# The wide two-operand operations of GpSimd in a two-layer block, moved to VectorE

## The chip, the cores and the metric

The kernel runs on one core of a Trainium2 chip. The metric is the time of one execution on the device in microseconds (us). The engines are named as the profile names them: PE is TensorE (its weight loads are listed apart as PEld), DVE is VectorE, ACT is ScalarE, POOL is GpSimd, SP is SyncE, which issues the DMAs of this kernel.

## The reference

The reference computes two layers over 1024 tokens of width 1024, in float32. Each layer has a mixing part and a gated feed-forward part; each part is normalised before and after, and scaled, shifted and gated by vectors that come from a conditioning vector `c`.

```python
for layer in range(DEPTH):                       # 2
    shift, scale, gate = adaln_params(c, ada_w[layer, 0], ada_b[layer, 0])
    h = rms_norm(x, norm_pre[layer, 0]) * (1.0 + scale) + shift
    if layer % 2 == 0:
        y = delta_rwkv_mixer(h, ...)             # 4 gated-delta heads of 128, 8 RWKV-7 heads of 64
    else:
        y = rglru_mixer(h, ...)                  # a gated linear recurrence of width 1024
    x = x + gate * rms_norm(y, norm_post[layer, 0])
    ...
    y = swiglu_ffn(h, ffn_w_gate[layer], ffn_w_up[layer], ffn_w_down[layer])   # width 2816
    x = x + gate * rms_norm(y, norm_post[layer, 1])
```

In the delta mixer a triangular system of a chunk is solved for every head; the kernel does it by a product form of the inverse.

## The kernel before

**Split products.** PE's fast float32 product rounds its operands. So each operand that needs the full precision is kept as two tiles, a rounded one (`wh`, `xh`) and the rest (`wl = w - wh`), and a product is three matmuls: `wh*xh + wh*xl + wl*xh`. A weight tile of 128 x 512 therefore takes a DMA (`wf` or `wd`), a copy on ACT that rounds (`nc.scalar.copy(wh, wf)`, line 144) and a two-operand subtraction (line 145 in `load_w`). Lines 677 and 678 in `parts` do the same in the feed-forward part.

**Who subtracts.** In `load_w` it is POOL while `self.pool_lo` is set: 2 during the whole mixer (every tile), True in the recurrence `lru` (only tiles with `k0 > 0`); else DVE. Weights that come a second time (the second half of the tokens) are not split again: the two parts were written to DRAM (`self.pd`) and are read back by DMA. In the feed-forward part `first(f)` gives its two splits to POOL, all other `parts` go to DVE.

**The mixer** (`mixer`): two halves of 512 tokens, and in each 8 groups of heads. A group goes through three stages (`inputs`, `first`, `second`), and the stages of three neighbouring groups are issued together, by counts. Every `first` calls `inverse` once. There, `L`, `Z` (lines 1198, 1200) are made on DVE, `X` is copied on POOL (line 1202), and `im = first + one32` is a sum on POOL (line 1204). `im` is used once, after the last level of the inverse. In the first half weights come in and are split; in the second half they are read back. `mix_out` for the first half is issued at step `MIX0`, inside the second half.

**The feed-forward part** (`ffn`): for each of 22 blocks `f` of the hidden width, seven products of 12 matmuls in the manner of Strassen. `first(f)` makes the two products that need only `ffn_w_gate`; some of them are made ahead, before and while `operands` prepares the sums and differences of the activations on DVE and ACT. Then `rest` goes through the blocks: `second(f)`, `first(f+1)`, `third(f)`.

**Order.** Only the start of the program fixes the order on DVE and PE by hand. In all else the order of instructions on each engine is made by a planner from the order of the program, the dependences, free buffers and the durations that it expects. On the chip each engine then runs its own list strictly in that order.

Of the kernel before, what the change touches and what calls it, by code (L numbers as in the profile page):

```python
# [15 lines left out]
ALU = mybir.AluOpType  # L16
# [56 lines left out]
class Block:  # L73
# [53 lines left out]
    def load_w(self, w, c0, nk=KD, n=128, tag=None, key=None):  # L127


        nc = self.nc  # L130
        step = 512 // n
        out = []
        for k0 in range(0, nk, step):
            m = min(step, nk - k0)
            wh = self.t(tag or "wh", [128, step, n], F32R)[:, :m]
            wl = self.t(tag or "wl", [128, step, n], F32R)[:, :m]
            kept = self.wparts.get((key, c0, k0))
            if kept is not None:
                for x, r in zip((wh, wl), kept):
                    nc.sync.dma_start(x.bitcast(F32).rearrange("p k c -> p (k c)"), r)  # L140
            else:
                wf = self.t(next(self.wtags), [128, step, n])[:, :m]
                nc.sync.dma_start(wf, w[k0 * 128:(k0 + m) * 128, c0:c0 + n].rearrange("(k p) c -> p k c", p=128))
                nc.scalar.copy(wh, wf)  # L144
                (nc.gpsimd if self.pool_lo and (self.pool_lo > 1 or k0) else nc.vector).tensor_tensor(wl, wf, wh, ALU.subtract)  # L145
                if key is not None:
                    kept = []
                    for x in (wh, wl):
                        r = self.pd[len(self.wparts) * 256 + len(kept) * 128:][:128, :m * n]
                        nc.sync.dma_start(r, x.bitcast(F32).rearrange("p k c -> p (k c)"))  # L150
                        kept.append(r)
                    self.wparts[key, c0, k0] = kept
            out += [(wh[:, k], wl[:, k]) for k in range(m)]
        return out
# [38 lines left out]
    def run(self):  # L193
        nc, a = self.nc, self.a
        self.pools = {}
        self.bg = iter(())
        self.abufs = iter(())
        self.held = False
        self.wtags = cycle(("wf",))
        self.pool_lo = False  # L200
        self.c = self.pool("const")
        main = self.pool("main")
        self.tags(main, wf=2, wh=3, wl=3, ht=16, yx=9, sm1=6, ss=8, e=8, jk=1)
        psum = self.pool("psum", PSUM)
        self.tags(psum, mm=2, es=1, sa=3, sb=2)
        x1, x2, x3, mT = [self.dram(n) for n in ("x1", "x2", "x3", "mT")]
        self.gd = self.dram("gd", 2 * NF * 2 * 128, 512)
        self.pd = self.dram("pd", 132 * 256, 512)
        self.wparts = {}
        self.cd = self.dram("cd", 2 * (PRE + MID) * 128, 512)  # L210
        with ExitStack() as self.ctx:
            self.tags(self.pool("start"), a0=6, k0=12, k1=1, wab=1)
            E = mybir.EngineType
            with self.tc.manual_schedule(engines={E.DVE, E.PE}):
                hs, AB, others = self.start()
            others()
            self.setup_constants()
            self.mixer_params(a["mix_w_in"][0])
        with ExitStack() as self.ctx:
            self.tags(self.pool("work"), p=12, ar=2, s1=8, cy=12, s2=4, st=2, gb=2, ad=4)  # L220
            rest = self.ctx
            with ExitStack() as self.ctx:
                self.tags(self.pool("mix"), W=2, h16=5, ch=4, sg=2, gp=4, egc=3, **{f"S{i}": 1 for i in range(8)})
                hs, AB, late = self.mixer(a["x"][0], x1, mT, hs, AB)
            self.ctx = rest
            self.tags(self.pool("deep"), wd=6)
            self.layers(hs, AB, x1, x2, x3, late)
# [431 lines left out]
    def ffn(self, l, hs):  # L659
# [4 lines left out]
        nc, a = self.nc, self.a  # L664
# [4 lines left out]
        flat = lambda x: x.rearrange("p k c -> p (k c)")  # L669
        b11, b21 = hs[:4], hs[4:]  # L670
        b22, t1, t2, t3, t4 = ([] for _ in range(5))
        kept = {}

        def parts(full, eng=None):
            wh = self.t("wh", [128, 4, 128], F32R)
            wl = self.t("wl", [128, 4, 128], F32R)
            nc.scalar.copy(flat(wh), full)  # L677
            (eng or nc.vector).tensor_tensor(flat(wl), full, flat(wh), ALU.subtract)  # L678
            return wh, wl

        def product(ps, w, xs, start):
            wh, wl = w
            for k in range(4):
                xh, xl = xs[k]
                self.mm(ps, wh[:, k], xh, start=start and k == 0, stop=False, more=not start)
                self.mm(ps, wh[:, k], xl, start=False, stop=False, more=not start)
                self.mm(ps, wl[:, k], xh, start=False, stop=k == 3, more=not start)
# [10 lines left out]
        def first(f, away=False):  # L698

            a11, a12 = fetch("ffn_w_gate", f)  # L700
            pa = self.t("mm", [128, 512])
            product(pa, parts(a11, nc.gpsimd), b11, True)
            c1 = E()
            nc.scalar.copy(c1, pa)  # L704
            product(pa, parts(a12, nc.gpsimd), b21, False)
            s0 = E()
            self.act(s0, pa, AF.Silu)
            kept[f] = [(lambda x=x: x) for x in (c1, s0)]
            if away:
                for n, x in enumerate((c1, s0)):  # L710
                    nc.sync.dma_start(self.cpart(f, n), x)
                    kept[f][n] = lambda n=n: self.back(f, n)
# [82 lines left out]
        def rest(ahead, late):  # L795
            following(0)
            for f in range(NF):
# [4 lines left out]
                if f >= late:  # L802
                    self.tick()

        return first, operands, rest

    def cpart(self, f, n):
# [89 lines left out]
    def layers(self, hs, AB, x1, x2, x3, late):  # L897
# [4 lines left out]
        for n, (l, x_in, x_out) in enumerate(subs):  # L902
# [7 lines left out]
            if l is not None:  # L910
                first, operands, rest = self.ffn(l, hs)
# [12 lines left out]
            for h in range(2):  # L924
                keep = h == 1 and l is None
                if l is None:
                    self.pool_lo = True
                    ys, w = self.lru(h, hs)
                    self.pool_lo = False
                    lhs = lambda k, half: ys[k]  # L930
                else:
                    w = self.a["ffn_w_down"][l]
                    for f in range(AHEAD if h == 0 else 0):
                        gs[0, f] = self.load_g(0, f)

                    def lhs(k, half):
                        if half == 0 and h == 0 and k + AHEAD < NF:
                            gs[0, k + AHEAD] = self.load_g(0, k + AHEAD)
                        g = gs[h, k]
                        if half == 1 and h == 0 and k >= 2:  # L940
                            gs[1, k - 2] = self.load_g(1, k - 2)
                        return g

                    if h == 1:
                        for f in (NF - 2, NF - 1):
                            gs[1, f] = self.load_g(1, f)
                nxt = []

                def aside():
                    if h == 0:  # L950
                        if l is None:
                            nxt.append(self.prenorm(x_in, 1, *AB))
                    elif n + 1 < len(subs):
                        while "A" not in res[n + 1] or n == 0 and len(res[1]["G"]) < 2:
                            self.tick()
                        nxt.append((res[n + 1]["A"], res[n + 1]["B"]))
                        nxt.append(self.prenorm(x_out, 0, *nxt[0]))

                last = n + 1 == len(subs) and h == 1
                xs = self.down(lhs, w, h, x_in, x_out, res[n]["G"], F_BANKS[4:] + F_BANKS[:4],  # L960
                               "s2" if keep else "yx", ("cy", 6) if keep else ("ht", 7) if last else (None, 0), keep, aside,
                               "lru" if l is None else None)
                if nxt:
                    hs = nxt[-1]
                    if h:
                        AB = nxt[0]


    def mixer(self, x, x_out, mT, hs, AB):
        nc, a, c = self.nc, self.a, self.c  # L970
# [5 lines left out]
        self.gW, self.rW = self.t("W", [128, 4, 128], F16), self.t("W", [128, 8, 64], F16)  # L976
        for W in (self.gW, self.rW):
            nc.gpsimd.memset(W, 0.0)
        self.pool_lo = 2
        groups = [(h, i) for h in range(2) for i in (0, 4, 1, 5, 2, 6, 3, 7)]  # L980
        one, two = {}, {}
        half = {}
# [22 lines left out]
        for n in range(len(groups) + 2):  # L1005
# [23 lines left out]
            for kind, res in zip(kinds, self.together(tasks)):  # L1029
                if kind == 1:  # L1030
                    two[n - 1] = res
                elif kind == 0:
                    one[n] = res
        self.pool_lo = False
        return hs, AB, lambda: self.mix_out(1, x, x_out, mT, r0["G"], F_BANKS)

    def mix_out(self, h, x, x_out, mT, Gb, banks):
# [148 lines left out]
    def inverse(self, lev, tri, first, one16, one32, ones, prod, shape, W, turn):  # L1186
# [6 lines left out]
        nc = self.nc  # L1193
# [7 lines left out]
        X = self.t("h16", shape, F16)  # L1201
        nc.gpsimd.tensor_copy(X, one16)
        im = self.t("s1", shape)
        nc.gpsimd.tensor_tensor(im, first, one32, ALU.add)
        for n in range(len(lev)):
            nb, s = N >> (n + 1), 1 << n
            runs = lambda x, e: x.rearrange("p c (b e s) -> p c b e s", e=2, s=s)[:, :, :, e]
# [366 lines left out]
```

## Time and profile before

| | |
|---|---|
| time of three runs | 2735.04, 2748.76, 2749.45 us, median 2748.76 |
| profiled execution | 2738.0 us, span 2736.2 us, mean granted TensorE clock 0.989 |
| PE, PEld | 2618.2 us (96% of the span), 2030.5 us (74%) |
| DVE, ACT, POOL | 1814.0 us (66%), 1178.8 us (43%), 336.9 us (12%) |

The span runs from the first to the last instruction; 1.8 us of the profiled time lie around it. Busy time is the union of an engine's instructions; PE's ends are modelled, so that a busy PE may still be waiting inside. In the order of the span: the start (to about 50 us), the mixer's first half of tokens (to about 450), its second half with the output product of the first (to about 960), the feed-forward of layer 0 (to about 1700), the recurrence (to about 2020), the feed-forward of layer 1.

### The profile page before, as it was taken

The page shows a single profiled execution, that of the slowest core. Times are in us where ns is not written, and L with a number is a line of the kernel's source. Part 1 is how long each engine was busy: PE and PEld are TensorE (multiplying, and loading weights), DVE is VectorE, ACT ScalarE, POOL GpSimd, SP SyncE. Part 2 cuts the span into 40 slices and gives each one's busy share as a digit, 9 for nine tenths or more (in the row PEclk, how much of TensorE's full clock was granted, in tenths as well). Part 3 has the DMA queues.
Part 4 walks back from the last instruction along what each step waited for, and adds up shares of the span by engine and source line. Part 5 has one row for each costly group of instructions (what it writes and reads, how often), then busy time and mean ns, then how long its engine had stood idle before and what let it go on. Part 6 is the DMA issues. An engine that isn't in the chain of part 4 may idle for free. (4 is left out here: it accounts for less than half of the span.)

```text
span 2736.2 us, 44054 instructions
## 1 busy us (share of the span) xinstructions
PE 2618.2 (96%) x16104; PEld 2030.5 (74%) x16104; DVE 1814.0 (66%) x3376; ACT 1178.8 (43%) x2164; POOL 336.9 (12%) x288
## 2 busy tenths in 40 slices
PE   6899999999999998999999999999998999999998
PEld 3666667676766666788888878777876888888887
DVE  5677777668776655997664473995855976664233
ACT  3555564554455525333332233573645333332222
POOL 2332220002111113000110000210012001110000
PEclk9999999999999999999999999999999999999999
DMA  7644442336832374775448884889655754448753
GB/s 244 225 132 140 139 154 79 110 105 231 274 107 83 97 250 157 247 233 188 135 148 306 300 273 140 293 299 299 201 197 166 227 178 148 135 135 289 247 177 110
DMA packets 423327, 519.60 MB, mean 190 GB/s; under 512 B 32667, under 2 KB 217790, under 8 KB 423110
## 3 DMA queue, kind: packets, MB, share of 16 engines
q1 hardware_dynamic: 423110, 516.78, 57.2%
q8 instruction: 127, 2.08, 0.3%
q14 instruction: 90, 0.74, 0.1%
HBM read 367.76 MB, written 148.90 MB: 189 GB/s over the span
## 5 line engine op out<-in xcount | busy, mean ns | idle before, releaser
L98 PE MATMUL mm<-ht,wh 128*128 128x512 f32 x1920 | 656.6, 415 | 19.1 <-ACT e L704 15.8
L98 PEld LDWEIGHTS mm<-ht,wh 128*128 128x128 f32 x1920 | 351.7, 191 | 107.7 <-ACT e L704 26.8
L98 PE MATMUL mm<-ht,wl 128*128 128x512 f32 x960 | 389.9, 408 | 11.4 <-DMA wl<-pd 5.9
L145 DVE TENSOR_TENSOR wl<-wd,wh 128x512 fp32r<-128x512 f32 x156 | 107.5, 690 | 177.9 <-ACT wh L144 175.7
L98 PEld LDWEIGHTS mm<-ht,wl 128*128 128x128 f32 x960 | 183.1, 191 | 55.0 <-DMA wl<-pd 6.8
L144 ACT CAST wh<-wd 128x512 fp32r<-128x512 f32 x168 | 104.4, 622 | 268.5 <-PE sb L98 216.9
L144 ACT CAST wh<-wf 128x512 fp32r<-128x512 f32 x133 | 82.3, 622 | 166.1 <-PE sb L98 78.5
L145 POOL TENSOR_TENSOR wl<-wf,wh 128x512 fp32r<-128x512 f32 x80 | 115.5, 1450 | 298.4 <-ACT wh L144 211.7
L678 POOL TENSOR_TENSOR wl<-wd,wh 128x512 fp32r<-128x512 f32 x60 | 78.0, 1299 | 580.0 <-ACT wh L677 379.5
L106 ACT ACTIVATE e<-mm 128x512 f32<-128x512 f32 x120 | 71.6, 597 | 136.0 <-PE mm L98 131.7
L555 POOL TENSOR_TENSOR sm<-sm,dv 128x1 f32<-128x1 f32 x64 | 40.5, 642 | 679.8 <-DVE sm L553 345.2
L98 PE MATMUL sa<-s,wh 128*128 128x512 f32 x392 | 122.1, 393 | 0.0
L677 ACT CAST wh<-wd 128x512 fp32r<-128x512 f32 x99 | 61.7, 623 | 127.8 <-issue 37.1
L106 ACT ACTIVATE e<-e 128x512 f32<-128x512 f32 x140 | 88.3, 633 | 57.9 <-DVE e L1098 27.0
L106 ACT ACT_TABLE_LOAD x84 | 107.8, 1283 | 2.2 <-PEq L1563 0.7
L98 PEld LDWEIGHTS <-h 64*64 64x64 f16 (+1 forms) x1984 | 53.4, 106 | 71.8 <-issue 47.6
L677 ACT CAST wh<-yx 128x512 fp32r<-128x512 f32 x88 | 54.6, 621 | 101.5 <-PE sa L98 42.1
L677 ACT CAST wh<-e 128x512 fp32r<-128x512 f32 x88 | 54.5, 619 | 98.9 <-PE sa L98 43.7
L98 PE MATMUL sa<-wh,p 128*128 128x512 f32 x260 | 92.6, 399 | 0.0
L678 DVE TENSOR_TENSOR wl<-e,wh 128x512 fp32r<-128x512 f32 x88 | 60.5, 687 | 44.2 <-ACT wh L677 44.2
L98 PEld LDWEIGHTS sa<-s,wh 128*128 128x128 f32 x392 | 74.4, 190 | 15.5
L145 DVE TENSOR_TENSOR wl<-wf,wh 128x512 fp32r<-128x512 f32 x53 | 36.5, 690 | 69.2 <-ACT wh L144 67.2
(495 smaller groups left out, 6482.2 us busy)
## 6 DMA issues: line engine op xcount, KB each, us to landing
gd<-yx SPq DMA_DIRECT2D x176, 256.0 KB, 2.3
pd<-wh SPq DMA_DIRECT2D x132, 256.0 KB, 2.4
pd<-wl SPq DMA_DIRECT2D x132, 256.0 KB, 2.9
wd<-in_ffn_w_down_dram SPq DMA_DIRECT2D x132, 256.0 KB, 3.6
wh<-pd SPq DMA_DIRECT2D x120, 256.0 KB, 2.6
wl<-pd SPq DMA_DIRECT2D x120, 256.0 KB, 2.9
wd<-in_ffn_w_gate_dram SPq DMA_DIRECT2D x114, 256.0 KB, 2.8
wd<-in_ffn_w_up_dram SPq DMA_DIRECT2D x78, 256.0 KB, 3.0
```

The costliest lines, as they stand in the source:

```text
L98: self.nc.tensor.matmul(out, lhsT=lhsT, rhs=rhs, start=start, stop=stop, skip_group_check=more)
L106: return self.nc.scalar.activation(out, in_, func, bias=bias, scale=scale)
L144: nc.scalar.copy(wh, wf)
L145: (nc.gpsimd if self.pool_lo and (self.pool_lo > 1 or k0) else nc.vector).tensor_tensor(wl, wf, wh, ALU.subtract)
L555: nc.gpsimd.tensor_tensor(r, r, self.mhalf[:, 0:1], ALU.pow)
L677: nc.scalar.copy(flat(wh), full)
L678: (eng or nc.vector).tensor_tensor(flat(wl), full, flat(wh), ALU.subtract)
```

## The change

Every two-operand subtraction of a weight split and the sum of the inverse go from POOL to DVE. The flag `pool_lo` and the argument `eng` of `parts` fall away. The rounding copies stay on ACT, the copy of `X` (line 1202), the power of the norms (line 555, one column) and four splits of the start (line 111) stay on POOL.

```diff
@@ load_w
-                (nc.gpsimd if self.pool_lo and (self.pool_lo > 1 or k0) else nc.vector).tensor_tensor(wl, wf, wh, ALU.subtract)
+                nc.vector.tensor_tensor(wl, wf, wh, ALU.subtract)
@@ run, layers, mixer
-        self.pool_lo = False
...
-                    self.pool_lo = True
...
-        self.pool_lo = 2
@@ ffn
-        def parts(full, eng=None):
+        def parts(full):
...
-            (eng or nc.vector).tensor_tensor(flat(wl), full, flat(wh), ALU.subtract)
+            nc.vector.tensor_tensor(flat(wl), full, flat(wh), ALU.subtract)
...
-            product(pa, parts(a11, nc.gpsimd), b11, True)
+            product(pa, parts(a11), b11, True)
...
-            product(pa, parts(a12, nc.gpsimd), b21, False)
+            product(pa, parts(a12), b21, False)
@@ inverse
-        nc.gpsimd.tensor_tensor(im, first, one32, ALU.add)
+        nc.vector.tensor_tensor(im, first, one32, ALU.add)
```

## Rows read from the trace of the kernel before

**Rows 1.** The page, part 1: busy time, share of the span, instructions of each engine.

```profile
PE 2618.2 (96%) x16104; PEld 2030.5 (74%) x16104; DVE 1814.0 (66%) x3376; ACT 1178.8 (43%) x2164; POOL 336.9 (12%) x288
```

**Rows 2.** Windows: length, busy us of PE, PEld, DVE, ACT, POOL, clock, DMA.

```profile
50.00:420.00 370.00, 343.98 (x3199) 243.28 (x3196) 282.60 (x583) 208.97 (x401) 109.95 (x80) 0.99 0.49 160
640.00:700.00 60.00, 57.20 (x318) 42.93 (x318) 48.91 (x85) 17.81 (x39) 17.77 (x13) 0.98 0.82 283
1060.00:1100.00 40.00, 30.29 (x123) 23.68 (x122) 37.52 (x55) 22.82 (x40) 5.72 (x5) 0.87 0.46 145
1100.00:1500.00 400.00, 398.19 (x1757) 326.54 (x1756) 290.61 (x449) 135.23 (x227) 20.69 (x16) 1.00 0.63 208
1700.00:1900.00 200.00, 183.01 (x804) 147.71 (x803) 162.62 (x308) 109.28 (x187) 30.80 (x27) 0.98 0.87 294
2090.00:2125.00 35.00, 25.29 (x96) 19.38 (x96) 33.00 (x50) 17.52 (x31) 3.19 (x3) 0.85 0.49 155
```

**Rows 3.** Groups of POOL by shape: xcount, busy us, mean ns, idle before.

```profile
L145 POOL TENSOR_TENSOR wl<-wf,wh 128x512 fp32r<-128x512 f32 x80 | 115.5, 1450 | 298.4 <-ACT wh L144 211.7 <-PE mm L98 32.6 <-PE sb L98 17.2
L678 POOL TENSOR_TENSOR wl<-wd,wh 128x512 fp32r<-128x512 f32 x60 | 78.0, 1299 | 580.0 <-ACT wh L677 379.5 <-DMA gd<-yx 199.5 <-DMA cd<-e 1.0
...
L678 POOL TENSOR_TENSOR wl<-wf,wh 128x512 fp32r<-128x512 f32 x28 | 36.9, 1318 | 317.5 <-ACT wh L677 315.9 <-PE mm L98 1.6
L1204 POOL TENSOR_TENSOR s<-s,k 128x512 f32<-128x512 f32 x16 | 24.8, 1551 | 328.6 <-DVE s L1447 157.5 <-DVE ch L1515 106.0 <-DVE s L1266 65.1
L145 POOL TENSOR_TENSOR wl<-wd,wh 128x512 fp32r<-128x512 f32 x12 | 18.2, 1514 | 155.2 <-ACT wh L144 142.8 <-DMA pd<-wl 8.4 <-DVE wl L145 4.0
L1202 POOL COPY h<-k 128x512 f16<-128x512 f16 x16 | 17.1, 1070 | 0.0
```

**Rows 4.** Groups of DVE by shape: two of one operation and shape.

```profile
L678 DVE TENSOR_TENSOR wl<-e,wh 128x512 fp32r<-128x512 f32 x88 | 60.5, 687 | 44.2 <-ACT wh L677 44.2
...
L747 DVE TENSOR_TENSOR yx<-wd,wd 128x512 f32<-128x512 f32 x39 | 43.5, 1115 | 0.6 <-DMA wd<-in_ffn_w_up_dram 0.6
```

**Rows 5.** Timeline, one meeting of POOL and DVE: start us, us, instruction.

```profile
2305.60 1.29 POOL L678 TENSOR_TENSOR wl<-wd,wh 128x512 fp32r<-128x512 f32 x1 [1.43 <-ACT wh L677]
2305.69 1.75 DVE L747 TENSOR_TENSOR yx<-wd,wd 128x512 f32<-128x512 f32 x1
```

**Rows 6.** Windows of line 145 alone: its busy us and count by engine.

```profile
50.00:420.00 370.00, 0.00 (x0) 86.14 (x60) 0.99 0.49 160
640.00:700.00 60.00, 0.00 (x0) 16.11 (x12) 0.98 0.82 283
1700.00:1900.00 200.00, 26.78 (x39) 23.27 (x15) 0.98 0.87 294
```

**Rows 7.** Waits of PE: who, for whom, us in total, times, longest.

```profile
PE sa L98 <- DVE wl L145: 6.1, 4, 2.3
PE mm L98 <- POOL wl L145: 6.0, 7, 2.5
...
PE sa L98 <- DVE h L1198: 3.6, 5, 1.1
```

**Rows 8.** Waits of DVE, the longest in total.

```profile
DVE wl L145 <- ACT wh L144: 242.9, 126, 6.6
```

**Rows 9.** Timeline of POOL: the sums of the inverses, the first, 8th, 11th, 13th, 16th.

```profile
95.79 2.34 POOL L1204 TENSOR_TENSOR s<-s,k 128x512 f32<-128x512 f32 x1 [2.56 <-DVE s L1266]
...
450.98 1.68 POOL L1204 TENSOR_TENSOR s<-s,k 128x512 f32<-128x512 f32 x1 [43.19 <-DVE s L1447]
...
613.55 1.70 POOL L1204 TENSOR_TENSOR s<-s,k 128x512 f32<-128x512 f32 x1 [50.84 <-DVE ch L1515]
...
763.50 1.28 POOL L1204 TENSOR_TENSOR s<-s,k 128x512 f32<-128x512 f32 x1 [2.34 <-DVE s L1266]
...
903.77 1.64 POOL L1204 TENSOR_TENSOR s<-s,k 128x512 f32<-128x512 f32 x1 [19.29 <-DVE s L1447]
```

More of the change, by code (lines that the diff above doesn't have):

```diff
@@ L926, in layers @@
                 if l is None:
-                    self.pool_lo = True
                     ys, w = self.lru(h, hs)
-                    self.pool_lo = False
                     lhs = lambda k, half: ys[k]
@@ L1033, in mixer @@
                     one[n] = res
-        self.pool_lo = False
         return hs, AB, lambda: self.mix_out(1, x, x_out, mT, r0["G"], F_BANKS)
```

## The prediction

> **What bounds the kernel now.** I read the page's engine table first. PE is busy for 96% of the span, DVE for 66%, POOL for 12% [rows 1]. The reader should see two things: POOL, the engine that loses work, has almost nothing to do, and DVE, which gets it, is not the engine with the longest busy time. So a change of DVE's or POOL's total alone moves nothing; what counts is where PE stands idle because of one of them.
>
> The windows come next, because one mean hides stretches with different limits. In the mixer's first half (50 to 420 us) PE is idle for 370 - 344.0 = 26.0 us, in the output product (640 to 700) for 2.8, in the recurrence (1700 to 1900) for 17.0, and in two short stretches where `operands` prepares the activations (1060 to 1100 and 2090 to 2125) for 9.7 each. In these two DVE is busy for 37.5 of 40 and 33.0 of 35 us: there DVE sets the pace. In the steady feed-forward (1100 to 1500) PE is idle for 1.8 of 400 us, and DVE is free for more than a quarter of the time [rows 2]. So the change can show in the mixer, in the recurrence and in those 75 us, and nowhere else.
>
> Then the groups of POOL: 80 + 12 splits of line 145, 60 + 28 of line 678 and 16 sums of line 1204 leave it, 196 instructions that take 115.5 + 18.2 + 78.0 + 36.9 + 24.8 = 273.4 us, 1.39 us each. The 16 copies of line 1202 stay [rows 3]. Then the groups of DVE, for the price of the same instruction there (0.687 us), and for something that the diff doesn't show: line 747 is a subtraction or sum of the same shape, and its 39 instructions take 1.115 us on average [rows 4]. The timeline says why. A POOL split starts at 2305.60 and runs to 2306.89; the DVE instruction that starts at 2305.69 takes 1.75 us, which is the rest of POOL's instruction (1.20) and some 0.55 of its own [rows 5]. POOL's work is thus not free for DVE today. Last, the waits of PE: those that a POOL split ended sum to 6.0 us in 7 waits [rows 7].
>
> **What the change does to DVE.** It adds 196 x 0.687 = 134.7 us. It takes away the meetings with POOL. From below that is 39 x (1.115 - 0.687) = 16.7 us, which line 747 alone shows; from above it is the whole 273.4 us for which POOL was busy with these instructions. For a value: a POOL instruction that starts while DVE is busy (76% of the time in the first half, 282.6 of 370) holds the next DVE instruction for about half of its own length: 196 x 0.70 x 0.76 = 104 us, an estimate. So DVE goes from 1814 to 1814 + 135 - 104 = 1845 us, between 1675 and 1932. Most of what is "moved to DVE" was already being paid by DVE, as waiting.
>
> The Trainium skill ("SBUF — State Buffer", section "Who interferes with whom") states the stronger form: a DVE instruction with two SBUF inputs and a GpSimd instruction that reads SBUF exclude each other for the whole instruction. The meeting above agrees with it. By that rule the relief could reach its upper end and DVE would end near 1675 us, which still is not PE's time.
>
> **Terms on PE's path**, against the profiled execution's 2738.0 us:
>
> Waits for POOL's weight parts, 6.0 us. A split on DVE takes 0.69 instead of 1.45 us, but it queues behind other DVE work. I take -4; the ends are 0 and -6.0.
>
> The sum of the inverse. POOL's sum and DVE's line 1198 start from the same tile at the same time; PE waits for line 1198 for 3.6 us in 5 waits [rows 7]. The copy of line 1202 still can meet it. Against that, 16 x 0.687 = 11.0 us come into DVE's list ahead of the first predicated copy of each inverse; DVE would otherwise wait there for PE's first small product, and PE has projections of another group to do. I take -1, between -3.6 and +11.0.
>
> The two stretches that DVE paces hold 5 + 3 POOL instructions, all splits of `first` [rows 2]: 8 x 0.687 = +5.5, less 8 x 0.65 (half a split) x 0.94 (DVE's busy share) = 4.9 of meetings. I take +1; the ends are +5.5 (no relief) and 5.5 - 8.9 = -3.4 (all of POOL's 5.72 + 3.19). The granted clock there is 0.87 and 0.85, so part of it ran at the lower level, 1.2 GHz; a longer idle stretch would keep it there longer, which leans this term to the costly end.
>
> The recurrence: 15 splits [rows 6], +10.3 us on a DVE that is busy for 162.6 of 200 us, less, in the same way, 15 x 0.78 x 0.81 = 9.5. PE already waits 6.1 us for DVE's splits there [rows 7]. I take +1, between -6.1 and +10.3.
>
> The mixer's first half gets 60 splits [rows 6] and 7 sums, 46.0 us: DVE would go from 282.6 to 328.6 of 370 us (89%) without relief, and stay near 76% with it (67 x 0.70 x 0.76 = 36 us, and up to 97). The 12 splits of the output product add 8.2 us to 48.9 of 60. I take 0 for both, and the reason is the best evidence that I found. The sums of the inverses mark the groups. From the first to the eighth, with weights split on POOL, 355.2 us pass for 7 groups, 50.7 each. In the second half the weights are read back and POOL splits almost nothing: 162.6 us for 3 groups and, past the output product, 140.3 for 3 more, 50.5 each [rows 9]. So the splits and all their meetings do not slow the groups by anything one can see; whatever is gained by ending them is small. The cover is PE's own work; if it is gone, the bound is the 89%.
>
> In the steady feed-forward 16 splits add 11.0 us to DVE's 290.6 of 400 under a PE that never stops: 0. If this cover were gone it would cost those 11.0.
>
> Sum: 2738.0 - 4 - 1 + 1 + 1 = 2735 us. The profiled execution is at the low end of what was seen: the three runs are 3.0 below, 10.8 and 11.5 above it, and the mean of the four is 2743, 5 above. I forecast 2735 + 5 = 2740 us, 0.3% under the median shown. About 0.5% (13.7 us) is what a measurement of this kernel can tell from no change.
>
> **Rivals.**
>
> Faster, about 2718 us: the mixer is not paced by PE's own work but by chains through DVE that the meetings lengthen, in both halves alike. PE's idle time in the five stretches is 26.0 + 2.8 + 9.7 + 17.0 + 9.7 = 65.2 us; if a third of it goes, 22 us, that gives 2740 - 22. For it speaks that most of the relief falls in the mixer; against it, that the second half is no quicker without POOL's splits. Weight loads fill 243.3 of 370 us (66%) in the mixer and 326.5 of 400 (82%) in the steady feed-forward, at matmul busy shares of 93% and over 99% [rows 2]; the mixer may have room that its idle time does not show, and so the case gets more than a small chance. The Trainium skill ("Perfetto Trace Analysis", section "Identifying the Most-Contended Engine") says that matmul busy time is a poor measure of how full PE is and that the share of weight loads is a better one; by it the mixer's room would be some 370 x (1 - 66/82) = 72 us instead of 26, an estimate, and a third of that would give about 2716 us.
>
> Slower, about 2764 us: DVE's strict list. A split now stands in it and waits for ACT's rounding copy, with the inverse's predicated copies and the recurrent steps behind it; before, POOL waited, and nobody stood behind. Where DVE does such splits already, it waits for ACT 242.9 us in 126 waits, 1.9 us each [rows 8]. There are 72 splits in the first half and the output product; if each delays PE by 0.33 us, that is 24 us. It decides from 0.31 us for each split: 0.5% above the median shown is 2762.5 us, 22.5 above my forecast. Against it: ACT is busy for only 209 of 370 us there, so its copies are seldom late, and the planner puts a split where it expects the copy to be done.
>
> No effect but a new order: the planner makes the whole list anew from other durations, so that small waits move about everywhere. That has no sign; it widens the forecast by some 10 us on both sides.
>
> **Chances.** My forecast, with its own range of 2728 to 2755, 0.57; the faster rival 0.24; the slower 0.19. The range is 2712 to 2768: it takes in both rivals' times with a few us beyond each, and leaves out their far halves, two in ten together. Faster by over 0.5% 0.24, within 0.5% 0.57, slower 0.19.
>
> **What would show it.** Right: POOL's busy time falls to about 337 - 273 = 64 us, DVE's rises to 1845; line 747 falls to 0.69 us; no wait of PE is ended by a POOL split; the groups still pass in 50 to 51 us; PE's idle time in 1060 to 1100 and 2090 to 2125 stays within 3 us of 9.7. Wrong towards faster: groups of 48 us or less in both halves. Wrong towards slower: groups of 53 us or more in the first half alone, with DVE's waits for line 144 grown in the mixer, and PE waiting for lines 1214 and 1221. If DVE's busy time grows by over 100 us, the meetings were not what lengthened its instructions.

## The result, and the profile after

The changed kernel takes 2711.95 us (median of 4 runs, 2706.52 to 2717.74) beside 2749.11 us for the kernel before (4 runs, 2735.04 to 2753.57). The ratio is 0.9885, with a 95% interval of 0.9861 to 0.9909: faster by 1.15%, about 37 us by the medians. The forecast was 2740 us with most of the chance on no change; the time lies outside the forecast's own range, beyond the faster rival's 2718, and just under the low end of 2712 of the whole range. The profiled execution of the changed kernel took 2710.24 us with a span of 2708.4 us, 27.8 us less than the profiled one of before, which was at the low end of its runs. What follows compares these two spans, so it explains 27.8 us.

Part 1 of the page of the changed kernel, as in [rows 1]:

```profile
PE 2615.3 (97%) x16104; PEld 2027.5 (75%) x16104; DVE 1819.9 (67%) x3572; ACT 1178.4 (44%) x2166; POOL 56.8 (2%) x92
```

The groups of POOL and of DVE by shape, as in [rows 3, 4]; lines are now one to five lower (747 is 746, 1198 is 1193, 1204 is 1199):

```profile
L1197 POOL COPY h<-k 128x512 f16<-128x512 f16 x16 | 11.2, 699 | 608.5 <-ACT cy L1219 353.4 <-ACT s L1219 255.1
```

```profile
L145 DVE TENSOR_TENSOR wl<-wf,wh 128x512 fp32r<-128x512 f32 x133 | 91.3, 687 | 84.6 <-ACT wh L144 81.4 <-DMA yx<-x 2.0 <-DMA wf<-in_ffn_w_down_dram 1.1
...
L746 DVE TENSOR_TENSOR yx<-wd,wd 128x512 f32<-128x512 f32 x39 | 26.7, 684 | 0.0
```

POOL lost 280.1 us. DVE got 196 instructions, 134.7 us at 0.687 us each, and is busy for only 5.9 us more. Busy time is a union, and DVE instructions that follow each other overlap by some 0.08 us in the records, so what DVE was relieved of is read from the durations instead: added up one by one, they went from 1996.5 to 2014.7 us, 18.2 more, so 134.7 - 18.2 = 116.5 us are gone from the old instructions. Line 746 shows where: the same 39 instructions fell from 1115 to 684 ns. Before, 131 DVE instructions took over 0.25 us more than the median of their operation and shape, 111.8 us in all, and 128 of them overlap a POOL instruction of over 0.9 us; such an overlap is called a meeting below. After, 11 are left, with 5.1 us.

Windows of the stages of [rows 2] (length, busy us of PE, PEld, DVE, ACT, POOL, clock, DMA share, GB/s); the two short stretches and the recurrence are shifted, because they now come earlier:

```profile
50.00:420.00 370.00, 361.63 (x3405) 257.14 (x3403) 293.39 (x694) 218.35 (x426) 10.13 (x14) 0.98 0.50 162
640.00:700.00 60.00, 54.93 (x315) 40.97 (x314) 45.40 (x95) 18.34 (x37) 2.09 (x4) 1.00 0.85 286
1042.00:1082.00 40.00, 33.40 (x145) 25.56 (x145) 38.22 (x64) 24.99 (x44) 0.00 (x0) 0.96 0.47 147
1100.00:1500.00 400.00, 399.91 (x1767) 328.56 (x1766) 286.12 (x458) 136.83 (x232) 0.00 (x0) 1.00 0.65 216
1675.00:1875.00 200.00, 186.81 (x814) 151.15 (x813) 159.93 (x326) 113.25 (x194) 7.10 (x12) 0.97 0.88 298
2058.00:2093.00 35.00, 28.57 (x118) 20.88 (x117) 33.76 (x56) 20.93 (x39) 0.00 (x0) 0.95 0.45 145
```

PE's idle time in the first half fell from 26.0 to 370 - 361.63 = 8.4 us, in the two stretches of `operands` from 9.7 and 9.7 to 6.6 and 6.4, in the recurrence from 17.0 to 13.2, in the steady feed-forward from 1.8 to 0.1; in the output product it rose from 2.8 to 5.1.

PE's waits (who, for whom, us, times, longest), and the two longest of DVE, as in [rows 7, 8]:

```profile
PE sa L98 <- DVE wl L145: 3.9, 2, 2.0
...
PE mm L98 <- DVE wl L677: 2.3, 4, 1.1
...
PE mm L98 <- DVE wl L145: 1.2, 1, 1.2
```

```profile
DVE wl L145 <- ACT wh L144: 254.4, 145, 7.0
DVE wl L677 <- ACT wh L676: 122.3, 63, 3.4
```

The 6.0 us that POOL's splits cost PE are gone; 3.5 us of waits for DVE's splits are new, and the old one fell from 6.1 to 3.9. DVE's own waiting for ACT's casts grew, for line 145 from 242.9 to 254.4 us, and for `parts` to 122.3 us.

I cut both spans at marks that exist in both: the first rounding copy of the mixer's first group (end of the start), the 16th line 1198 (head of the last group's inverse), the first line 615 on the last four tiles of the first feed-forward part, and the last pair of scans of the recurrence.

| stage | before | after | difference, us |
|---|---|---|---|
| start | 67.7 | 68.5 | +0.8 |
| mixer | 838.9 | 820.2 | -18.7 |
| feed-forward of layer 0 | 792.5 | 787.2 | -5.3 |
| recurrence | 288.7 | 285.6 | -3.1 |
| feed-forward of layer 1 | 748.4 | 746.9 | -1.5 |

These are one profile of each kernel. The changed kernel, profiled once more beside the last experiments, took 818.7 us in the mixer, 790.0 and 743.1 in the two feed-forward parts and 284.7 in the recurrence. The mixer's gain is far beyond this scatter; those of the feed-forward parts are of its size.

Two thirds of the gain are in the mixer, and there in its first half: from its first group's mark to the same mark of the second half 396.3 us became 373.8. The second half, up to the 16th line 1198, went the other way, from 442.6 to 446.5 us. Windows of the mixer, first of the kernel before, then of the changed one; the first row is the first two groups (up to the second line 1198), the second row the rest of the mixer:

```profile
67.70:150.20 82.50, 71.87 (x395) 53.16 (x396) 59.65 (x109) 43.82 (x85) 32.50 (x24) 0.96 0.68 222
150.20:906.60 756.40, 734.10 (x7303) 522.51 (x7302) 561.91 (x1235) 404.64 (x785) 124.85 (x95) 1.00 0.42 137
```

```profile
68.50:136.70 68.20, 64.61 (x376) 47.84 (x375) 56.07 (x124) 43.41 (x84) 2.21 (x4) 1.00 0.79 256
136.70:888.70 752.00, 738.17 (x7306) 525.71 (x7304) 558.80 (x1307) 402.37 (x786) 15.09 (x22) 0.99 0.42 138
```

The first two groups alone gave 82.5 - 68.2 = 14.3 us, the other fourteen 4.4 (8.3 in the rest of the first half, less the 3.9 of the second). Not all of the 14.3 us is waiting: the order changed, and the window holds 395 matmuls before and 376 after. PE's idle time in it fell by 7.0 us, from 82.5 - 71.87 = 10.6 to 68.2 - 64.61 = 3.6, and its busy time by 7.3. In the first two, only one or two tasks run beside each other, and PE has little other work to turn to. Groups of DVE by shape in the window of these two groups, before and after:

```profile
L480 DVE SCALAR_TENSOR_TENSOR ad<-ad,sc,ad 128x512 f32<-128x512 f32 x7 | 6.1, 874 | 1.3 <-DMA ad<-in_ada_w_dram 1.3
L1083 DVE COPY tails<-e 128x3 f32<-128x3 f32 x8 | 3.6, 448 | 3.4 <-ACT e L106 3.4
...
L1174 DVE TENSOR_TENSOR p<-e,e 128x512 f32<-128x512 f32 x1 | 1.8, 1759 | 0.0
...
L1261 DVE TENSOR_TENSOR s<-s,s 128x512 f32<-128x512 f32 x1 | 1.6, 1607 | 0.1
```

```profile
L479 DVE SCALAR_TENSOR_TENSOR ad<-ad,sc,ad 128x512 f32<-128x512 f32 x7 | 5.2, 746 | 0.1
...
L1078 DVE COPY tails<-e 128x3 f32<-128x3 f32 x7 | 1.1, 161 | 0.1
...
L1169 DVE TENSOR_TENSOR p<-e,e 128x512 f32<-128x512 f32 x1 | 0.7, 685 | 0.0
...
L1256 DVE TENSOR_TENSOR s<-s,s 128x512 f32<-128x512 f32 x1 | 0.7, 684 | 0.0
```

The instructions at lines 1174 and 1261 are single steps of a chain. Beside a POOL split they took 1759 and 1607 ns; now they take 685 and 684. The second of these meetings, before:

```profile
76.69 1.51 POOL L145 TENSOR_TENSOR wl<-wf,wh 128x512 fp32r<-128x512 f32 x1 [1.85 <-ACT wh L144]
77.15 1.61 DVE L1261 TENSOR_TENSOR s<-s,s 128x512 f32<-128x512 f32 x1
```

### The profile page after: what moved, and what is told of

Same layout as the page of the kernel before. It is cut to its first block, busy times and chain, and to the rows that moved or that the text cites. A ratio compares the mean times of both kernels' runs of the same rounds, so it can differ in the third digit from the quotient of the medians.

```text
span 2708.4 us, 43886 instructions
## 1 busy us (share of the span) xinstructions
PE 2615.3 (97%) x16104; PEld 2027.5 (75%) x16104; DVE 1819.9 (67%) x3572; ACT 1178.4 (44%) x2166; POOL 56.8 (2%) x92
## 5 line engine op out<-in xcount | busy, mean ns | idle before, releaser
L98 PE MATMUL mm<-ht,wh 128*128 128x512 f32 x1920 | 646.9, 411 | 17.5 <-ACT e L703 10.8
L145 DVE TENSOR_TENSOR wl<-wd,wh 128x512 fp32r<-128x512 f32 x168 | 115.7, 689 | 179.2 <-ACT wh L144 173.1
L145 DVE TENSOR_TENSOR wl<-wf,wh 128x512 fp32r<-128x512 f32 x133 | 91.3, 687 | 84.6 <-ACT wh L144 81.4
L677 DVE TENSOR_TENSOR wl<-wd,wh 128x512 fp32r<-128x512 f32 x99 | 67.7, 686 | 60.4 <-ACT wh L676 60.4
L676 ACT CAST wh<-e 128x512 fp32r<-128x512 f32 x88 | 54.4, 618 | 100.3 <-DVE e L747 48.9
L98 PE MATMUL mm<-wh,p 128*128 128x512 f32 x216 | 78.3, 402 | 6.0 <-ACT wh L144 4.6
L98 PEld LDWEIGHTS sb<-ch,cy 64*64 64x64 f32 (+1 forms) x640 | 48.7, 144 | 43.9 <-issue 13.1
```

Of the source, the lines that this page charges most:

```text
L98: self.nc.tensor.matmul(out, lhsT=lhsT, rhs=rhs, start=start, stop=stop, skip_group_check=more)
L145: nc.vector.tensor_tensor(wl, wf, wh, ALU.subtract)
L677: nc.vector.tensor_tensor(flat(wl), full, flat(wh), ALU.subtract)
```

## The experiments

All ratios below are to the kernel before, run on the same chip (medians of 2744.0 to 2745.4 us there). Mixer times are those of the stage table, from one profile each. The changed kernel itself was run again beside the last ones: 0.9870 (0.9854 to 0.9885), 2709.61 us, mixer 818.7.

### One part at a time

**a_mix_splits**: the kernel before, but the mixer's weight splits go to DVE.

```diff
-        self.pool_lo = 2
```

> The kernel before with only the weight splits of the mixer (72 in its first half of tokens and the output product, a few more later) moved to VectorE; the inverses' sums, the feed-forward's and the recurrence's splits stay on GpSimd. The first half of the mixer (from the scalars of the first half to those of the second) took 396 us before and 374 us after. Theory M (meetings: GpSimd's splits hold VectorE's two-input instructions, and these delay TensorE): most of the 22 us goes, first half 376 to 382 us, ratio to before 0.992 to 0.995. Theory L (latency: what counts is only that a weight part is ready 0.8 us earlier): the same run looks the same, it is told apart by the shadow run. Theory S (the sum of the inverse meeting line 1198 at the head of each inverse): little goes, first half 390 us or more, ratio 0.998 to 1.000.

**b_sums**: the kernel before, but the sum of the inverse goes to DVE.

```diff
-        nc.gpsimd.tensor_tensor(im, first, one32, ALU.add)
+        nc.vector.tensor_tensor(im, first, one32, ALU.add)
```

> The kernel before with only the 16 sums of the inverses (line 1204) on VectorE. Theory S: first half of the mixer 380 us or less, ratio 0.993 to 0.995. Theory M or L: the 16 sums are a tenth of what POOL did in two-operand work; first half 390 to 396 us, ratio 0.998 to 1.001.

**c_ffn_lru**: the kernel before, but the splits of `first` and of the recurrence go to DVE.

```diff
-            product(pa, parts(a11, nc.gpsimd), b11, True)
+            product(pa, parts(a11), b11, True)
...
-            product(pa, parts(a12, nc.gpsimd), b21, False)
+            product(pa, parts(a12), b21, False)
...
-                    self.pool_lo = True
```

> The kernel before with only the 88 splits of the early products and the 16 of the recurrence on VectorE; the mixer as before. Between the marks of the two profiles these stages took some 10 us less after the whole change (2 to 5 us in the first feed-forward part, 4 in the recurrence, 3 to 5 in the second feed-forward part). If these gains are the stages' own: ratio 0.996 to 0.998. If they come from the changed order of a planner that starts from other states: ratio 0.999 to 1.001.

| kernel | ratio (95%) | median us | mixer | its first two groups | DVE busy |
|---|---|---|---|---|---|
| before | 1 | 2744.87 | 838.9 | 82.5 | 1814.0 |
| a_mix_splits | 0.9933 (0.9917 to 0.9950) | 2727.06 | 826.5 | 68.2 | 1814.0 |
| b_sums | 0.9989 (0.9977 to 1.0002) | 2740.78 | 835.1 | 80.7 | 1810.5 |
| c_ffn_lru | 0.9953 (0.9940 to 0.9966) | 2729.69 | 839.9 | 83.0 | 1823.7 |

The parts add up: 0.67 + 0.11 + 0.47 = 1.25%, beside 1.15 and 1.30% for the whole. The mixer's splits give more than half, the feed-forward and the recurrence most of the rest; the sum of the inverse gives nothing that is certain. The first half of the mixer, of which the expectations speak, took 396.3 us before, 375.2 in a and 390.2 in b; c gave more than the 0.2 to 0.4% that were expected of it. With a alone, the mixer's 76 splits on DVE left its busy time at 1814.0 us: the relief paid for all of them.

### Meetings, or something else that moved with the splits?

**d_shadow_pool**: the changed kernel, all its work in place. In the mixer POOL makes one more subtraction after each split, whose result nobody reads.

```diff
                 nc.vector.tensor_tensor(wl, wf, wh, ALU.subtract)
+                if self.extra:      # set for the mixer
+                    nc.gpsimd.tensor_tensor(wf, wf, wh, ALU.subtract)
```

> The changed kernel, and in the mixer each weight split is made once more by GpSimd, into the tile that the weights came in, whose content nobody reads afterwards. TensorE, VectorE and ScalarE have the same list of instructions in the same order as in the changed kernel; nobody waits for the second split but the next load into its buffer. Theory M: the meetings come back, VectorE's busy time in the mixer's first half rises by 30 us or more, the first half goes from 374 to 385 us or more, ratio to before 0.993 to 0.999. Theory L, S, or a better order as the cause: the first half stays within 4 us of 374, ratio 0.987 to 0.990.

Measured: 0.9964 (0.9950 to 0.9978), 2735.24 us. DVE's busy time rose by 41.2 us to 1861.1, with the same 3572 instructions, and the lists of PE, DVE and ACT are instruction for instruction those of the changed kernel, but for four small fills on DVE that change places with a neighbour (two do so between two profiles of the changed kernel itself). So no new order is in this number. The same windows for d (first two groups, rest):

```profile
73.90:152.90 79.00, 67.08 (x376) 48.72 (x375) 66.39 (x123) 43.56 (x84) 30.39 (x22) 0.98 0.68 217
152.90:914.00 761.10, 738.94 (x7306) 524.61 (x7305) 586.91 (x1306) 402.31 (x786) 94.91 (x78) 0.99 0.42 136
```

The mixer is back at 840.1 us (before: 838.9). With the same 376 matmuls in the window, the first two groups went from 68.2 to 79.0 us. The first half took 385.7 us (373.8 in the changed kernel) and the second 454.4 (446.5). DVE's busy time in the first half rose by 26.8 us, a little less than the 30 expected. One thing besides the meetings is in it: POOL holds `wf` longer, and SP's loads wait for it (47.3 us in 49 waits between 50 and 450 us). The next kernel has no such hold.

**f_meet_pool**: as d, but POOL's extra operation reads `wl` and `wh` and writes a scratch tile; no load waits for it.

```diff
+                if self.extra:
+                    j = self.t("jk", [128, step, n], BF16)
+                    nc.gpsimd.tensor_tensor(j[:, :m], wl, wh, ALU.add)
```

> The changed kernel, and in the mixer each weight split is followed by one more two-input instruction of the same size on GpSimd (the sum of the two parts, into a scratch tile that nobody reads). Other than in the earlier shadow run the tile that the weights came in is not held, so that no load waits for it. Theory M: the first half returns to 382 us or more, as in the shadow run (386), ratio 0.993 to 0.998. Theory Q (the SyncE queue: in the kernel before, and in the shadow run, a transfer in the queue waits for GpSimd, and the weight loads behind it are late): the first half stays within 4 us of 374, ratio 0.987 to 0.990.

**e_more_dve**: the same extra operation on DVE: the same load on it, but no meeting.

```diff
+                    nc.vector.tensor_tensor(j[:, :m], wl, wh, ALU.add)
```

> The changed kernel, and in the mixer each weight split is followed on VectorE by one more two-input instruction of the same size (the sum of the two parts, into a scratch tile that nobody reads): some 50 us of VectorE in all, no meeting. Theory V (VectorE's own time sets the pace of the mixer, so that 0.69 us costs there whoever causes it): the first half goes from 374 to 390 us or more, ratio to before 0.994 or more. Theory M (a meeting costs because it holds up an instruction for longer, and unplanned): the planner makes room for it, the first half grows by less than 8 us, ratio 0.988 to 0.991.

Windows of f, then of e (first two groups, rest):

```profile
69.20:146.90 77.70, 70.36 (x388) 52.35 (x389) 67.80 (x115) 40.08 (x73) 29.59 (x20) 0.96 0.73 238
146.90:907.70 760.80, 740.05 (x7309) 525.34 (x7308) 590.59 (x1322) 407.47 (x802) 97.19 (x81) 0.99 0.42 136
```

```profile
68.50:135.10 66.60, 63.33 (x360) 46.43 (x360) 59.82 (x122) 38.56 (x71) 1.24 (x1) 0.97 0.75 242
135.10:903.30 768.20, 746.83 (x7317) 534.34 (x7315) 592.99 (x1382) 408.45 (x804) 17.62 (x26) 0.98 0.42 136
```

| kernel | ratio (95%) | mixer | first two groups | rest | DVE busy, against after |
|---|---|---|---|---|---|
| after | 0.9870 (0.9854 to 0.9885) | 820.2 | 68.2 | 752.0 | |
| d_shadow_pool | 0.9964 (0.9950 to 0.9978) | 840.1 | 79.0 | 761.1 | +41.2 |
| f_meet_pool | 0.9945 (0.9929 to 0.9960) | 838.5 | 77.7 | 760.8 | +43.3 |
| e_more_dve | 0.9923 (0.9910 to 0.9936) | 834.8 | 66.6 | 768.2 | +41.3 |

So 76 POOL operations of 1.46 us, with nobody waiting for their results, cost 43.3 / 76 = 0.57 us of DVE each and bring back the whole loss of the mixer (18.3 of 18.7 us in f, 19.9 in d). What f lacks in return is the old order: its lists on PE, DVE and ACT differ from those of the changed kernel from about 60 us on. So d has the same order and a hold on `wf`, f no such hold and a new order, and both say the same. The groups of DVE in the first two groups of f show the lengthened instructions again:

```profile
L483 DVE SCALAR_TENSOR_TENSOR ad<-ad,sc,ad 128x512 f32<-128x512 f32 x7 | 8.6, 1234 | 0.1
...
L1262 DVE TENSOR_TENSOR s<-s,s 128x512 f32<-128x512 f32 x1 | 1.8, 1779 | 0.0
```

Kernel e adds as much DVE busy time (its 76 instructions take 52.7 us by their own durations) and costs somewhat less (0.53% over after, where d costs 0.94 and f 0.75%; the intervals of e and f overlap), and all of it in the rest of the mixer, none in the first two groups. Its order is not that of after, however: the planner knows of e's extra work and puts work elsewhere, while it cannot know of a meeting. Of the two expectations for e neither came in full: the first half took 390.4 us, as theory V had it, and the ratio lies between the two. What follows: time that is taken from DVE costs the mixer about 15 to 20 us for 41 to 43 of busy time, whoever takes it; in the first two groups only the meetings cost anything.

**i_late_part**: as d, but POOL makes the split again into `wl`, with the same value, so that PE must wait for POOL as it did before the change. With d it tells whether lateness of the part adds to the meetings.

```diff
+                    nc.gpsimd.tensor_tensor(wl, wf, wh, ALU.subtract)
```

> The changed kernel, and in the mixer GpSimd makes each weight split once more, into the same tile, so that TensorE waits for GpSimd's result as in the kernel before. To be set beside the shadow run, which has the same meetings and lacks only this lateness (first half and second to the mark of the sixteenth inverse: 840 us in the mixer, against 820 in the changed kernel and 839 before; ratio 0.9964). Theory L (the later part costs some 10 us by itself): the mixer takes 848 us or more, ratio 0.999 or more. Theory M alone: within 4 us of 840, ratio 0.995 to 0.998.

Measured: 0.9970 (0.9957 to 0.9983), 2737.07 us, mixer 841.9, first two groups 77.3. That is d's result within the intervals (0.9964 and 840.1). The planner gave i a new order too, from about 70 us on. That POOL's part is late adds nothing that can be seen.

**g_before_later** and **h_after_later**: the writes of the weight's parts to DRAM stand in SP's strict queue ahead of the next weight's load, and a late part holds them up: in the kernel before, SP waits there for POOL's parts for 109.7 us in 83 waits. Here they are held back until the next weight is loaded, in the kernel before (g) and in the changed one (h).

```diff
+                while self.unsent:
+                    nc.sync.dma_start(*self.unsent.pop(0))
...
-                        nc.sync.dma_start(r, x.bitcast(F32).rearrange("p k c -> p (k c)"))
+                        self.unsent.append((r, x.bitcast(F32).rearrange("p k c -> p (k c)")))
```

> The kernel before; the transfers that write a weight's two parts to DRAM are issued one weight tile later, behind the next tile's load, so that the SyncE queue does not wait for GpSimd's split in front of a load. Theory Q: the first half goes from 396 to 385 us or less, ratio 0.993 to 0.996. Theory M: within 4 us of 396, ratio 0.998 to 1.002.

> The changed kernel with the same later issue of the parts' transfers. Theory Q and theory M: little is left for the queue to give, first half within 5 us of 374, ratio to before 0.986 to 0.990. Tried also because it could beat the changed kernel, where weight loads still wait in the queue for a split.

Measured: g 1.0006 (0.9993 to 1.0018), mixer 847.2, first two groups 82.2; h 0.9867 (0.9855 to 0.9880), 2705.9 us, mixer 817.2. If a queue held up by POOL's late parts had cost the kernel before its time, g would have got it back. It got nothing. That theory falls.

### The feed-forward part, and a further step

**j_meet_ffn**: the changed kernel, with 88 unread POOL operations beside the splits of `first`, the number that the change took away there.

```diff
-            product(pa, parts(a11), b11, True)
+            product(pa, parts(a11, True), b11, True)
...
+            if meet:
+                nc.gpsimd.tensor_tensor(self.t("jk", [128, 512], BF16), flat(wl), flat(wh), ALU.add)
```

> The changed kernel, and in the two feed-forward parts each of the 88 splits of the early products is followed by one more two-input instruction of the same size on GpSimd (the sum of the two parts, into a scratch tile that nobody reads). Theory M (meetings in the stretches that VectorE paces): most of the 13 us that moving the feed-forward's and the recurrence's splits gave goes again, ratio to before 0.991 to 0.994. If those 13 us came from the earlier parts: ratio within 0.987 to 0.990.

Measured: 0.9958 (0.9941 to 0.9974), 2734.43 us, so 25 us above the changed kernel on the same chip, more than the 13 us (0.47%) that c gave and more than either expectation had. The mixer took 817.6 us, 1.1 less; the two feed-forward parts went from 790.0 and 743.1 us (the changed kernel profiled beside it) to 801.8 and 757.6. The two stretches from the first subtraction of `operands` to the first sum of `second` after it (line 762) took 44.7 and 44.9 us before, 40.2 and 40.9 after, 41.2 and 39.9 in c, and 48.9 and 46.7 in j. PE's longest waits around the first of them, in `first` (for a rounding copy, and for the copy that empties the first product), before (1040 to 1110 us) and after (1030 to 1090):

```profile
PE es L98 <- ACT wh L677: 5.2, 1, 5.2
PE mm L98 <- ACT e L704: 4.3, 2, 2.6
```

```profile
PE es L98 <- ACT wh L676: 2.9, 1, 2.9
PE mm L98 <- ACT e L703: 1.7, 2, 1.0
...
PE mm L98 <- DVE wl L677: 0.9, 2, 0.6
```

These waits fell from 5.2 + 4.3 to 2.9 + 1.7 us, and 0.9 us for DVE's splits, which POOL made before, is new.

One thing besides the meetings is in j: POOL's extra operation reads `wh` as well, and ACT's next rounding copies into that buffer wait for it. The same wait existed, much smaller, in the kernel before, and none is left after the change. ACT's waits for POOL, before and in j:

```profile
ACT wh L677 <- POOL wl L678: 4.6, 5, 1.4
```

```profile
ACT wh L676 <- POOL jk L679: 31.2, 13, 4.6
```

So j shows that POOL's work beside `first` costs time in these stretches, but not how much of it is meetings. TensorE's granted clock moved too: over the two stretches as cut here it was 0.89 and 0.89 before, 0.96 and 0.96 after, 0.83 and 0.89 in j.

**k_less_pool**: h, and two more kinds of wide POOL work gone: the copy of `X` to ACT, and the four splits of the start to DVE.

```diff
-                hs.append(self.split(full, "ht", nc.gpsimd if k % 2 else None))
+                hs.append(self.split(full, "ht"))
...
-        nc.gpsimd.tensor_copy(X, one16)
+        nc.scalar.copy(X, one16)
```

> The changed kernel with the parts' transfers issued one tile later (0.9867 when tried alone), and the rest of GpSimd's wide work gone too: the 16 copies at the head of the inverses on ScalarE, the four splits of the start on VectorE. Theory M: GpSimd's copies still take 11 us and meet VectorE's first instructions of each inverse, which gives 2 to 6 us; ratio to before 0.983 to 0.987. If the copies do not matter: 0.986 to 0.990.

**l_after_again**: the changed kernel, beside k.

> The changed kernel itself, on the same chip as the three others, for the comparison: ratio 0.987 to 0.990.

Measured: k 0.9837 (0.9820 to 0.9855), 2700.54 us (2696.47 to 2704.53), beside 2709.61 (2707.38 to 2711.13) for the changed kernel: no run of k is as slow as the fastest of the other. It is the best version. But its gain is not where its edits act: the mixer takes 818.7 us in both, and the feed-forward of layer 0 takes 779.5 beside 790.0, where the edits put no more than the last copy of `X`. A new order from the planner is the likely cause; no run here shows it.

## Why the prediction was wrong

**The mixer, taken at 0, was -18.7 us.** This is the step that failed. The prediction's "best evidence" was that groups pass at 50.7 us with POOL's splits and at 50.5 without them, so that the splits and their meetings do not slow the groups. The timeline of DVE after the change, at the sums that were [rows 9]:

```profile
91.46 0.68 DVE L1199 TENSOR_TENSOR s<-s,k 128x512 f32<-128x512 f32 x1
...
428.26 0.69 DVE L1199 TENSOR_TENSOR s<-s,k 128x512 f32<-128x512 f32 x1
...
597.23 0.69 DVE L1199 TENSOR_TENSOR s<-s,k 128x512 f32<-128x512 f32 x1
...
750.29 0.68 DVE L1199 TENSOR_TENSOR s<-s,k 128x512 f32<-128x512 f32 x1
...
889.30 0.68 DVE L1199 TENSOR_TENSOR s<-s,k 128x512 f32<-128x512 f32 x1
```

The first half now takes (428.26 - 91.46) / 7 = 48.1 us a group, the second (169.0 + 139.0) / 6 = 51.3. So the two halves are not alike without the splits; their equal pace was chance. The 50.5 us of before was itself the mean of 54.2 us for the three groups ahead of the output product and 46.8 for the three past it. The second half reads two parts for each weight and has the output product among its groups; it was no measure of what the first half would be without meetings. d and f bring meetings back, and the mixer returns to 838 to 840 us: that meetings cost the mixer this much is shown; whether they are all that the change gained there stays open (below). The faster rival had this mechanism, but put it "in both halves alike": the first half gained 22.6 us, the second lost 3.9.

**The relief was 116.5 us, where 104 was estimated**, inside the bounds of 16.7 and 273.4. The chance that a POOL instruction starts under a busy DVE and then holds it for half its length came to 0.38 of POOL's time; measured is 116.5 / 273.4 = 0.43. This term was nearly right. DVE's busy time ended at 1819.9 and not at 1845 us: 12.5 us of the difference are the larger relief, the rest that overlap of some 0.08 us, by which an added instruction raises the union by less than its 0.687 us. The rule of the Trainium skill ("SBUF — State Buffer", section "Who interferes with whom"), that the two exclude each other for the whole instruction, agrees with the lengthened instructions seen here (1759 beside 685 ns); the sum is under half of POOL's time, in a span for two thirds of which DVE was busy [rows 1].

**The two stretches and the recurrence, +1 each, were -8.5 and -3.1 us.** The two stretches, for which the prediction had one term with a lower end of -3.4, became 4.5 and 4.0 us shorter; what left with POOL's splits was worth more there than the new work, where both were taken as nearly equal. j, with POOL's work brought back, makes the stretches longer than before; c, with none left there, as short as after. Three things left together and were not told apart: the meetings, ACT's waits for POOL's splits (1.7 us in each stretch), and a granted clock of 0.89 that rose to 0.96. For the recurrence alone nothing was run; in c, which moved its splits too, it took 288.4 us, as long as before, so the cause of the 3.1 us is open.

**Waits for POOL's weight parts, -4**: 6.0 gone, 3.5 new, 2.2 less at line 145's old wait, -4.7 in all. Right. **The sum of the inverse, -1**: b gives -3.0 us, from -6.3 to +0.5. Right within its interval.

**The slower rival did not come.** DVE does wait longer for ACT's casts (254.4 and 122.3 us), but the instructions behind a waiting split were not late for PE: no wait of PE is ended by line 1214 or 1221, and the predicated copy next to the latter (1222) ended 0.9 us in 2 waits. On the contrary, PE's waits for the inverse's instructions on DVE all but went: besides the 3.6 us for line 1198 [rows 7], the kernel before had

```profile
PE sa L98 <- DVE h L1221: 3.2, 6, 1.1
PE sa L98 <- DVE h L1214: 3.2, 2, 1.6
```

and of these 10.0 us only the 0.9 are left. PE runs other groups meanwhile, as the prediction had said of the inverse.

**The signs that were forecast:** POOL fell to 56.8 us (64), line 747 to 0.684 us (0.69), no wait of PE is ended by POOL, and the stretches' idle time came to 6.6 and 6.4 (9.7, within 3, just missed). "Groups of 48 us or less" came in one half.

**Two views spoke for it and were given too little weight.** PE's idle time of 26.0 us in the first half, of which 17.6 are gone from the same 370 us. And the weight loads' share, 66% there and 82% in the steady feed-forward: the Trainium skill ("Perfetto Trace Analysis", section "Identifying the Most-Contended Engine") reads the room from that share. It gave some 72 us of room; 22.6 us of it came true in the first half (396.3 to 373.8), and the share is now 257.14 / 370 = 0.695.

**What stays open.** Price times DVE time doesn't close. By durations added up, d and f put 40.1 and 47.4 us on DVE in the mixer for 19.9 and 18.3 us of mixer, 0.50 and 0.39 us for each, and e 50.7 us for 14.6, 0.29 for each. The changed kernel has 85 more DVE instructions between the mixer's marks, 58.4 us, and 61.7 us less of the old ones. At those prices that is a gain of 7 to 14 us, an estimate, and 18.7 were measured. The added work may have cost less than e's on top of it, or the new order gained something; no run tells. And the first two groups of d, f and i stay 3.5 to 5 us under the 82.5 of before, whose window holds 19 matmuls more than d's; how much of that is order was not separated.

## What to carry to other kernels

An idle engine is not a free helper when its instructions lengthen those of a busy one: before giving it work, or leaving it there, compare the mean time of one form of instruction with and without the helper beside it, and look for single instructions of twice the usual time inside short chains. Price it where PE has nothing else to do: here, with the same lists of instructions, 10.8 of the 19.9 us that d's meetings cost the mixer lay in two of sixteen groups. And don't take equal paces of two stages with unlike work as proof that the difference between them is free; take the thing away in one stage instead.

## What the runs showed that I had not expected

POOL's meetings also lengthen DVE instructions that read only one operand: the copy of 128 x 3 numbers at line 1083 took 448 ns on average in the first two groups before, and 161 ns after. One by one they took 157 to 170 ns without a POOL split beside them, and 667 to 1232 with one:

```profile
138.60 1.73 POOL L145 TENSOR_TENSOR wl<-wf,wh 128x512 fp32r<-128x512 f32 x1
139.12 1.23 DVE L1083 COPY tails<-e 128x3 f32<-128x3 f32 x1
```

The predicated copies of line 1221, which read PSUM (`sa`), hardly changed: 428 ns before, 429 after.

POOL is slowed too: its copy of `X` (line 1202) took 1070 ns on average before and 699 after, the sum that stood right ahead of it on POOL now being on DVE. In f it takes 795 ns. Whether that is the meeting with line 1198 was not tried.

And a POOL operation of 1.39 us cost DVE 116.5 / 196 = 0.59 us of lengthened instructions, where DVE needs 0.687 us to do the same operation itself. Moving it to POOL saved DVE 0.09 us.
